# A hybrid encoder layer in which GpSimd sorts the attention's strided operand into groups of 512 columns

## The chip, the core and the metric

The kernel runs on one core of a Trainium2 chip. The metric is device microseconds of one execution. Matrix work runs on TensorE (PE; its weight loads are listed apart as PEld), elementwise work on VectorE (DVE), ScalarE (ACT) and GpSimd (POOL). Transfers are queued by SyncE (SP), by ACT and by POOL, and all of these queues end on the same 16 DMA engines. Every engine works through its own instructions in a fixed order.

## The reference, cut to what matters

One layer over 2048 tokens of width 1024: a projection, a gated linear attention (GLA, 4 heads), a dilated attention (8 heads of 64), an output projection and a mixture of 32 experts. The change touches the dilated attention only. Each head attends in three patterns, each a band of radius 64 inside classes of tokens that lie 1, 4 or 16 positions apart:

```
DILATED_PATTERNS = ((128, 1), (512, 4), (2048, 16))
for window, dilation in DILATED_PATTERNS:
    o, lse = _dilated_attention(qh, kh, vh, window, dilation)   # band inside each class i mod dilation
    outs.append(o); lses.append(lse)
w = softmax(stack(lses), axis=0)
o = einsum('pbsh,pbshd->bshd', w, stack(outs, axis=0))
```

## The kernel before, in words

Patterns are called p = 0, 1, 2 (steps of 1, 4 and 16 tokens). In each, 16 blocks of 128 queries see 256 keys (128 keys for p = 2). Queries and keys are kept with the 64 features on the partitions and the 2048 tokens along a row, in high and low parts of float32r, so that a class of p = 1 is every fourth element of a row and a class of p = 2 every sixteenth. `block(p, b)` gives the two views.

The work around the change has two stages.

The first stage (from about 240 to 757 us) computes the rest of the input projection and, in between, the maxima. `maxima(h)` goes through 24 pairs of blocks per head. A block of p = 0 or p = 1 takes two matmuls (L482, L483), a block of p = 2 one (L480); each has 128 stationary columns (the queries, `aq`) and 256 moving columns (the keys, `kk`). DVE adds a mask and takes the maximum (L490, L492), ACT sums the exponentials (L495). `pump` calls for these pairs between the matmuls of the projection (L150 to L152, L160 to L162), whose weights arrive as `wraw` and are cast by ACT (L141) and DVE (L142). POOL queues the stores of this stage and the loads of `aq` and `kk`.

The second stage (757 to about 1200 us) is the attention proper. `attention()` walks through 24 steps of two blocks per head. A step puts the mask into PSUM by a bf16 matmul (L619, L622) and adds four score matmuls (L625, L626), with the keys `ak`, `bk` stationary and the queries `aq`, `bq` moving; ACT takes the exponential (L630, L632); four steps later `att_values` multiplies by the values (L660). The GLA work is drawn in at 0.9 of its own steps per attention step: decay (L363 to L388, with POOL at L379), preparation (L750 to L763, POOL at L752), a scan (L781 to L788, on PE and DVE in turn) and the output (L802 to L852, with POOL at L835). At the end `wout_load` fetches the rows of the output projection through the buffers of `vt` (L587 to L590).

The source gives priorities by its order; the tile scheduler fixes at build time the order in which each engine works, by its own estimate of time. So a change of the source can move neighbours too.

Of the kernel before, what the change touches and what calls it, by code (L numbers as in the profile page):

```python
# [25 lines left out]
P = 128  # L26
# [64 lines left out]
def tile_trunk(ctx, tc, x, norm1_w, w_in, gfw, gfb, gbw, gbb, gnw, w_out, norm2_w, rgw, rgb, rew, reb,  # L91
# [73 lines left out]
    def duo(t, c):  # L165

        return t.rearrange("p (l c) -> p c l", c=16)[:, c - c % 2:c - c % 2 + 2, :]

    def block(p, b):

        if p == 2:
            return (lambda t: t[:, b::16]), (lambda t: duo(t, b)), am[:, 768:896], 0
# [3 lines left out]
        return (lambda t: t[:, c::st][:, P * j:P * j + P]), (lambda t: t[:, c::st][:, k0:k0 + 256]), \  # L176
            am[:, 256 * v:256 * v + 256], k0 * st // 16
# [44 lines left out]
    with ExitStack() as ca:  # L222
# [169 lines left out]
        with ExitStack() as c2:  # L392
            wp = c2.enter_context(tc.tile_pool(name="wp", bufs=2, reuse_waits="tile"))
            ev = c2.enter_context(tc.tile_pool(name="ev2", bufs=2, reuse_waits="tile"))
            lp = c2.enter_context(tc.tile_pool(name="lp", bufs=1, reuse_waits="tile"))
# [55 lines left out]
            sp = c2.enter_context(tc.tile_pool(name="sp", bufs=4, reuse_waits="tile"))  # L451
# [17 lines left out]
            def maxima(h):  # L469
                aq, kk = MX.pop(h)  # L470
                for p in range(3):
                    for b0 in range(0, 16, 2):
                        if p == 0 and b0 == 4 and h < 7:
                            maxima_load(h + 1)
                        ps = pS.tile([P, 512], F32, name="psS")
                        for i in range(2):
                            qa, ka, _, _ = block(p, b0 + i)
                            o = ps[:, i * 256:i * 256 + 256]
                            if p == 2:
                                T.matmul(o, qa(aq), kk[:, :, b0 + i::16], start=True, stop=True)  # L480
                            else:
                                T.matmul(o, qa(aq), ka(kk[:, 0]), start=True, stop=False)  # L482
                                T.matmul(o, qa(aq), ka(kk[:, 1]), start=False, stop=True)  # L483
                        for i in range(2):
# [9 lines left out]
                            je = sp.tile([P, 256], BF16, name="je", bufs=2)  # L494
                            A.activation(je[:, :n], st[:, :n], AF.Exp, bias=nm[:, col:col + 1], scale=-1.0,  # L495
# [23 lines left out]
            for n, (q, c0, nc_, dst, d0) in enumerate(jobs):  # L519
# [5 lines left out]
                if nc_ > 256 and q == 1:  # L525
                    lse = joint_lse(0, pS, lambda n: lp.tile([P, (192, 384, 384, 512)[n]], F32, name=f"lse{n}"))
# [20 lines left out]
    WO = []  # L547
    with ExitStack() as cb:
        vp = cb.enter_context(tc.tile_pool(name="vp", bufs=3, reuse_waits="tile"))
# [7 lines left out]
        BB = [[pb[e].tile([P, S], F32R, name=n) for n in ("bq", "bk")] for e in range(2)]  # L557
        for bq, bk in BB:
            for t, one in ((bq, 0.0), (bk, 1.0)):
# [1136 lines left out]
```

## Time and profile before

| | |
|---|---|
| median of 3 runs | 2322.67 us (2321.29 to 2323.6) |
| the profiled execution | 2324.34 us, span 2322.6 us |
| granted PE clock, mean | 0.954 |
| busy share PE, PEld, DVE, ACT, POOL | 91%, 74%, 61%, 55%, 44% |
| chain that ended last | PE 71%, DVE 13%, DMA 9% |

The span runs from the first to the last instruction, and the profiled execution lies 1.74 us over its span. The busy shares are means over stages with different limits. Ends of matmuls are modelled, so the pace of PE is read here from the starts: the distance from one weight load to the next is what one matmul costs in a dense stretch. [...]

### The profile page before, as it was taken

Reading aid. Unit: us, or ns where it says so; the run is one execution under the profiler, and the core shown is the slowest. Engines: PE = TensorE matmul, PEld = TensorE weight load, DVE = VectorE, ACT = ScalarE, POOL = GpSimd, SP = SyncE. Lnnn points to the kernel's source line nnn. Section 1 sums busy time; section 2 is a strip of 40 time slices with the busy share of each in tenths; the row PEclk is TensorE's granted clock in tenths of the full one; section 3 lists DMA queues with packets and bytes.
Section 4 is the critical chain, followed back from the end, with each engine's and each line's share of the span. In section 5 each row is a group of like instructions: output and inputs, shape, how many; then the busy total and the mean of one; then the engine's idle time right before and its main releaser. Section 6 shows DMA issues by size and latency. Waiting matters only on the chain.

```text
span 2322.6 us, 38346 instructions
## 1 busy us (share of the span) xinstructions
PE 2112.9 (91%) x13813; PEld 1710.3 (74%) x13813; DVE 1409.6 (61%) x2871; ACT 1281.8 (55%) x2286; POOL 1014.8 (44%) x602
## 2 busy tenths in 40 slices
PE   7999998989799799999979999588898999999975
PEld 6888897989799677878768887366665666666654
DVE  7865544545365373626434666479876777768676
ACT  5222666657486464747442333356665767676744
POOL 4766111020120111202020001388887998888866
PEclk9999999999999899999989999799999999999988
DMA  8745765575642969685454643688988999999973
GB/s 308 233 107 151 183 181 163 149 207 147 175 124 69 217 152 187 145 193 113 114 149 151 212 155 127 214 269 282 328 272 279 327 326 329 300 317 295 310 279 151
DMA packets 283475, 487.09 MB, mean 210 GB/s; under 512 B 77079, under 2 KB 155927, under 8 KB 276096
## 3 DMA queue, kind: packets, MB, share of 16 engines
q1 hardware_dynamic: 238512, 368.40, 51.1%
q0 software_dynamic: 29344, 110.03, 17.0%
q10 hardware_dynamic: 15424, 6.16, 1.1%
q8 instruction: 110, 1.80, 0.3%
q14 instruction: 85, 0.70, 0.1%
HBM read 392.01 MB, written 94.44 MB: 209 GB/s over the span
## 4 chain that ended last, share of the span: by engine, by line
PE 71%; DVE 13%; DMA 9%; issue 3%; ACT 2%; POOL 1%; SPq 1%; ACTq 0%; another core or an unknown queue 0%; DVEq 0%; POOLq 0%
DMA wraw<-in_w_in_dram 5%; PE pg L1315 4%; PE pg L1317 4%; PE pg L1316 4%; DVE wlo L991 4%; PE psm L161 3%; PE po L1302 3%; PE psm L150 3%; PE psm L152 3%; PE psm L162 3%; PE psm L151 3%; PE psm L160 3%; PE po L1076 3%; PE po L1074 3%; PE po L1078 3%
## 5 line engine op out<-in xcount | busy, mean ns | idle before, releaser
L991 POOL TENSOR_TENSOR wlo<-raw,whi 128x2048 fp32r<-128x2048 f32 x97 | 513.3, 5302 | 87.0 <-ACT whi L986 83.0
L991 DVE TENSOR_TENSOR wlo<-raw,whi 128x2048 fp32r<-128x2048 f32 x95 | 372.6, 3931 | 64.0 <-ACT whi L986 64.0
L986 ACT CAST whi<-raw 128x2048 fp32r<-128x2048 f32 x192 | 366.8, 1910 | 53.2 <-PE pg L1383 36.6
L161 PE MATMUL psm<-wl,uhi 128*128 128x256 f32 (+1 forms) x768 | 222.9, 291 | 1.1 <-DVE wl L142 1.1
L160 PE MATMUL psm<-wh,uhi 128*128 128x256 f32 (+1 forms) x768 | 222.7, 290 | 0.7 <-ACT wh L141 0.5
L162 PE MATMUL psm<-wh,ulo 128*128 128x256 f32 (+1 forms) x768 | 221.6, 289 | 0.0
L1315 PE MATMUL pg<-whi,xh 128*128 128x512 f32 x512 | 215.7, 421 | 0.7 <-ACT xh L141 0.7
L495 ACT ACTIVATE je<-st,nm 128x256 bf16<-128x256 f32 (+1 forms) x384 | 178.6, 466 | 52.3 <-DVE nm L492 50.3
L1317 PE MATMUL pg<-wlo,xh 128*128 128x512 f32 x512 | 204.7, 400 | 0.0
L1316 PE MATMUL pg<-whi,xl 128*128 128x512 f32 x512 | 204.3, 399 | 0.0
L630 ACT ACTIVATE pt<-psS 128x512 f32<-128x512 f32 x128 | 131.0, 1074 | 85.3 <-PE psS L626 46.1
L625 PE MATMUL psS<-aq,ak 128*128 128x256 f32 x384 | 172.2, 455 | 0.0
L142 DVE TENSOR_TENSOR wl<-wraw,wh 128x512 fp32r<-128x512 f32 (+1 forms) x140 | 100.6, 738 | 92.5 <-ACT wh L141 92.1
L150 PE MATMUL psm<-uhi,wh 128*128 128x512 f32 (+1 forms) x400 | 153.8, 388 | 0.3 <-ACT wh L141 0.3
L151 PE MATMUL psm<-ulo,wh 128*128 128x512 f32 (+1 forms) x400 | 153.5, 385 | 0.5 <-DVE ulo L142 0.5
L152 PE MATMUL psm<-uhi,wl 128*128 128x512 f32 (+1 forms) x400 | 152.6, 385 | 0.0
L160 PEld LDWEIGHTS psm<-wh,uhi 128*128 128x128 f32 x768 | 150.5, 196 | 1.6 <-ACT wh L141 1.0
L161 PEld LDWEIGHTS psm<-wl,uhi 128*128 128x128 f32 x768 | 150.3, 196 | 1.6 <-DVE wl L142 1.3
L162 PEld LDWEIGHTS psm<-wh,ulo 128*128 128x128 f32 x768 | 149.1, 194 | 0.0
L492 DVE CUSTOM_DVE_ANT_0 st<-psS,am 128x256 f32<-128x256 f32 x256 | 98.6, 421 | 82.9 <-PE psS L483 57.5
L626 PE MATMUL psS<-bq,bk 128*128 128x256 f32 x384 | 141.5, 374 | 0.0
L141 ACT CAST wh<-wraw 128x512 fp32r<-128x512 f32 (+1 forms) x144 | 85.1, 623 | 97.3 <-DMA wraw<-in_w_in_dram 85.6
(420 smaller groups left out, 5097.1 us busy)
## 6 DMA issues: line engine op xcount, KB each, us to landing
raw<-in_expert_w_gate_dram SPq DMA_DIRECT2D x128, 512.0 KB
raw<-in_expert_w_up_dram SPq DMA_DIRECT2D x128, 512.0 KB
raw<-in_expert_w_down_dram SPq DMA_DIRECT2D x64, 1024.0 KB
wraw<-in_w_in_dram SPq DMA_DIRECT2D x128, 256.0 KB
xt<-in_x_dram SPq DMA_DIRECT2D x32, 512.0 KB
aq<-s_q POOLq DMA_DIRECT2D x8, 1024.0 KB, 8.3
kk<-s_khi POOLq DMA_DIRECT2D x16, 512.0 KB, 13.4
ak<-s_khi SPq DMA_DIRECT2D x16, 512.0 KB
```

What stands on the lines that cost most here:

```text
L150: T.matmul(ps[:m, ts], wh[:, k, m0:m0 + m], uh[:, k, ts], start=(k == 0), stop=False)
L151: T.matmul(ps[:m, ts], wh[:, k, m0:m0 + m], ul[:, k, ts], start=False, stop=False)
L152: T.matmul(ps[:m, ts], wl[:, k, m0:m0 + m], uh[:, k, ts], start=False, stop=(k == KD - 1))
L160: T.matmul(ps[:, :n], uh[:, k, sl], wh[:, k, :n], start=(k == 0), stop=False)
L161: T.matmul(ps[:, :n], uh[:, k, sl], wl[:, k, :n], start=False, stop=False)
L162: T.matmul(ps[:, :n], ul[:, k, sl], wh[:, k, :n], start=False, stop=(k == KD - 1))
L495: A.activation(je[:, :n], st[:, :n], AF.Exp, bias=nm[:, col:col + 1], scale=-1.0, accum_out=zt[:, col:col + 1])
L986: (A.copy if high is A else high.tensor_copy)(hi, raw)
L991: low.tensor_tensor(lo, raw, f32(hi), op=ALU.subtract)
L1315: T.matmul(pgt[n], xh[:, k], hi[:, 2 * n + kk], start=(k == 0), stop=False)
L1316: T.matmul(pgt[n], xl[:, k], hi[:, 2 * n + kk], start=False, stop=False)
L1317: T.matmul(pgt[n], xh[:, k], lo[:, 2 * n + kk], start=False, stop=(k == KD - 1))
```

## The change

GpSimd copies the moving operand of p = 1 and p = 2 into a tile `grp` of 128 partitions, 2 parts and 512 columns, in which the columns of each class lie side by side. There are four groups per pattern and head: one class of p = 1 each, or four classes of p = 2. Matmuls then read their 256 moving columns contiguously. The stationary operand is read as before, every fourth or sixteenth element. In the first stage this is the keys (`in_order` in `maxima`), in the second the queries (`in_order(h, p, g)`, called two steps before the group is used). Each stage has two `grp` buffers.

So that a step stays within one group, the steps of p = 1 now take blocks (4c+1, 4c+2) and (4c, 4c+3) of one class, and p = 2 runs c = 0 to 7. Blocks 4c and 4c+3 have different masks, so every second step of p = 1 takes two mask matmuls of 256 columns instead of one of 512. The values of p = 2 are taken step by step.

To find room for `grp`: `st` has 3 buffers instead of 4 and the exponential is written over it (`je` is gone), the pool `lp` is gone (its use goes to `tab`), `lz` becomes an `oe` buffer, `vt` has 2 buffers instead of 3, and `aq`, `bq` become one tile `qq`. The DVE memset of `bq` (2 x 2048) is gone.

```
+                def in_order():
+                    if todo_:
+                        p, g = todo_.pop(0)
+                        ready[p, g] = t = pa.tile([P, 2, 512], F32R, name="grp")
+                        if p == 1:
+                            G.tensor_copy(t, kk.rearrange("p e (m c) -> p e c m", c=4)[:, :, g])
+                        else:
+                            G.tensor_copy(t.rearrange("p e (c l) -> p e c l", c=4),
+                                          kk.rearrange("p e (l c) -> p e c l", c=16)[:, :, 4 * g:4 * g + 4])
...
                 for p in range(3):
                     for b0 in range(0, 16, 2):
+                        if (p, b0) in ((0, 8), (0, 12)) or (p and b0 % 4 == 0):
+                            in_order()
...
-                                T.matmul(o, qa(aq), kk[:, :, b0 + i::16], start=True, stop=True)
+                                T.matmul(o, qa(aq), kg.rearrange("p e (c l) -> p e c l", c=4)[:, :, (b0 + i) % 4], start=True, stop=True)
                             else:
-                                T.matmul(o, qa(aq), ka(kk[:, 0]), start=True, stop=False)
-                                T.matmul(o, qa(aq), ka(kk[:, 1]), start=False, stop=True)
+                                for e in range(2):
+                                    T.matmul(o, qa(aq), (kg if p else kk)[:, e, near], start=(e == 0), stop=(e == 1))
...
-        vp = cb.enter_context(tc.tile_pool(name="vp", bufs=3, reuse_waits="tile"))
+        vp = cb.enter_context(tc.tile_pool(name="vp", bufs=2, reuse_waits="tile"))
...
+        def in_order(h, p, g):
+            qq = ATT[h][2]
+            ATT["grp", h, p, g] = t = vp.tile([P, 2, 512], F32R, name="grp", bufs=2)
+            if p == 1:
+                G.tensor_copy(t, qq.rearrange("p e (m c) -> p e c m", c=4)[:, :, g])
+            else:
+                for x in range(2):
+                    G.tensor_copy(t[:, :, 256 * x:256 * x + 256].rearrange("p e (y l) -> p e y l", y=2),
+                                  qq.rearrange("p e (l c) -> p e c l", c=16)[:, :, 8 * x + 2 * g:8 * x + 2 * g + 2])
...
-                T.matmul(sv[:, e], ks(ak), qs(aq), start=False, stop=False, skip_group_check=True)
-                T.matmul(sv[:, e], ks(bk), qs(bq), start=False, stop=True, skip_group_check=True)
+                for w, kt in enumerate((ak, bk)):
+                    T.matmul(sv[:, e], ks(kt), (qg if p else qq)[:, w, near], start=False, stop=(w == 1), skip_group_check=True)
...
+                    n = t % 24 - 6
+                    if n >= 0 and n % 2 == 0 and n < 16:
+                        in_order(h, 1 + n // 8, n // 2 % 4)
```

The build puts the copies into POOL's queue as follows. Around the first stores of the values in the first stage, POOL's rows before are these (`s_...` are scratch tensors in memory, `kk_1912` is one of the two key tiles):

```order
L413 DMA s_gq<-ef 128x512 x2
L413 DMA s_gk<-ef 128x512 x2
L448 DMA s_v<-et 128x4x256
L464 DMA aq<-s_q 128x2048
L135 DMA kk_1912<-s_khi 64x2048 x2
```

At the same place POOL's rows now read (the key tiles are called `kk_1909` and `kk_1910`, and L442 is the former L448):

```order
L476 COPY grp<-kk_1909 128x1024 x2
L442 DMA s_v<-et 128x4x256
L476 COPY grp<-kk_1909 128x1024 x2
L474 COPY grp<-kk_1910 128x1024
L135 DMA kk_1909<-s_khi 64x2048 x2
```

Copies now stand in front of the stores and behind them, in the one queue. In the second stage, at the output of the first GLA head and the decay of the second, POOL's rows before are these (`tab` holds the decay tables, `vr` the GLA norm):

```order
L363 DMA lr<-s_lr 96x512 x2
L379 TENSOR_TENSOR tab<-tab 128x512 x2
L363 DMA lr<-s_lr 96x512 x2
L835 TENSOR_TENSOR vr<-vr,mhalf 128x4
L379 TENSOR_TENSOR tab<-tab 128x512 x2
```

Now they are (L374 is the former L379, L864 the former L835):

```order
L589 COPY grp<-qq 128x1024
L374 TENSOR_TENSOR tab<-tab 128x512 x2
L358 DMA lr<-s_lr 96x512
L589 COPY grp<-qq 128x1024
L358 DMA lr<-s_lr 96x512
L864 TENSOR_TENSOR vr<-vr,mhalf 128x4
L592 COPY grp<-qq 128x2x256 x2
L374 TENSOR_TENSOR tab<-tab 128x512 x2
```

Here copies and GLA instructions stand in turn. On PE, a step of p = 2 in the same stage reads before (L619 the mask, L625 and L626 the scores, L660 the values of an earlier step):

```order
L660 MATMUL pso<-pt,vt 64x2x64
L619 LDWEIGHTS identb
L619 MATMUL psS<-am,identb 128x2x128
L625 MATMUL psS<-aq,ak 128x256
L626 MATMUL psS<-bq,bk 128x256
```

and now (L648 the mask, L657 the scores, L691 the values, L831 a GLA matmul):

```order
L691 MATMUL pso<-pt,vt 64x2x64 x4
L648 LDWEIGHTS identb
L648 MATMUL psS<-am,identb 128x2x128
L831 MATMUL psg<-qd,ki 64x64 x3
L657 MATMUL psS<-grp,ak 128x256
L657 MATMUL psS<-grp,bk 128x256
```

The scores of a step no longer follow its mask at once; other work is put between, and some scores of p = 2 stand in the next head's steps of p = 0.

## Rows read from the trace of the kernel before

**Rows 1.** Windows by stage: us, busy (instructions) of each engine, PE clock, DMA share, GB/s.
```profile
240.00:757.00 517.00, 478.92 (x3128) 460.21 (x3126) 265.89 (x1067) 332.43 (x1027) 85.53 (x110) 0.96 0.56 154
757.00:1200.00 443.00, 409.44 (x4431) 340.93 (x4431) 211.36 (x463) 253.83 (x432) 70.00 (x63) 0.95 0.70 155
1200.00:1217.00 17.00, 2.20 (x8) 1.43 (x8) 5.33 (x19) 3.67 (x5) 0.43 (x2) 0.54 0.89 256
```

**Rows 2.** Timeline of PEld, a pair of p = 1: start us, us, engine, line.
```profile
266.60 0.19 PEld L161 LDWEIGHTS psm<-wl,uhi 128*128 128x128 f32 x1
266.72 0.31 PEld L482 LDWEIGHTS psS<-kk,aq 128*128 128x128 f32 x1
266.94 0.33 PEld L483 LDWEIGHTS psS<-kk,aq 128*128 128x128 f32 x1
...
267.41 0.34 PEld L483 LDWEIGHTS psS<-kk,aq 128*128 128x128 f32 x1
267.65 0.21 PEld L162 LDWEIGHTS psm<-wh,ulo 128*128 128x128 f32 x1
267.86 0.21 PEld L160 LDWEIGHTS psm<-wh,uhi 128*128 128x128 f32 x1
```

**Rows 3.** Timeline of PEld, a pair of p = 2 in the first stage.
```profile
282.87 0.52 PEld L480 LDWEIGHTS psS<-kk,aq 128*128 128x128 f32 x2
283.29 0.20 PEld L160 LDWEIGHTS psm<-wh,uhi 128*128 128x128 f32 x1
283.49 0.21 PEld L161 LDWEIGHTS psm<-wl,uhi 128*128 128x128 f32 x1
```

**Rows 4.** Timeline of PEld, a strided step of the second stage.
```profile
922.43 0.29 PEld L625 LDWEIGHTS psS<-aq,ak 128*128 128x128 f32 x1
922.63 0.31 PEld L626 LDWEIGHTS psS<-bq,bk 128*128 128x128 f32 x1
...
923.06 0.32 PEld L626 LDWEIGHTS psS<-bq,bk 128*128 128x128 f32 x1
923.48 0.11 PEld L619 LDWEIGHTS <-identb 128*128 128x128 bf16 x1
```

**Rows 5.** Timeline of PEld, a contiguous step (p = 0) of the second stage.
```profile
934.80 0.19 PEld L625 LDWEIGHTS psS<-aq,ak 128*128 128x128 f32 x1
934.92 0.19 PEld L626 LDWEIGHTS psS<-bq,bk 128*128 128x128 f32 x1
935.15 0.10 PEld L619 LDWEIGHTS <-identb 128*128 128x128 bf16 x1
```

**Rows 6.** Chain that ended last, second stage: start us, us, what.
```profile
754.72 1.78 DVE bq L561
...
845.11 5.61 issue
850.72 1.29 POOL tab L379
...
950.16 5.64 issue
```

**Rows 7.** Single lines: instructions, ns min/median/max, first and last start us.
```profile
L443 POOL TENSOR_TENSOR et<-et,nw x8: 2332/2404/2462, 229.8 to 654.5; 128x1024 f32<-128x1024 f32 x8
L560 POOL MEMSET bq<- x2: 1801/1804/1808, 605.5 to 752.4; 64x2048 f32 x2
L991 POOL TENSOR_TENSOR wlo<-raw,whi x97: 4495/5167/6696, 1439.6 to 2246.0; 128x2048 fp32r<-128x2048 f32 x97
L142 DVE TENSOR_TENSOR wl<-wraw,wh x140: 616/689/2501, 22.2 to 728.2; 128x512 fp32r<-128x512 f32 x124, 128x576 fp32r<-128x576 f32 x16
```

**Rows 8.** Waits: who waited for whom, us in total, times, longest us.
```profile
ACT wh L141 <- DMA wraw<-in_w_in_dram: 69.2, 22, 15.5
...
POOL vr L835 <- DVE vr L834: 74.1, 12, 16.2
```

**Rows 9.** Timeline at the end of the second stage, SP and DVE.
```profile
1201.30 1.41 SPq L587 DMA_DIRECT2D vt<-in_w_out_dram  x1
1208.50 1.23 DVE L590 TENSOR_TENSOR bk<-vt,bk 128x1024 fp32r<-128x1024 f32 x1 [2.77 <-ACT bk L589]
```

More of the change, by code (lines that the diff above doesn't have):

```diff
@@ L470, in maxima @@
                 aq, kk = MX.pop(h)
+                todo_ = [(p, g) for p in (1, 2) for g in range(4)]
+                ready = {}
+                def in_order():
[7 more added lines that the diff above has]
+                                          kk.rearrange("p e (l c) -> p e c l", c=16)[:, :, 4 * g:4 * g + 4])
                 for p in range(3):
                     for b0 in range(0, 16, 2):
+                        if (p, b0) in ((0, 8), (0, 12)) or (p and b0 % 4 == 0):
+                            in_order()
+                        kg = ready.get((p, b0 // 4))
                         if p == 0 and b0 == 4 and h < 7:
@@ L587, in wout_load @@
             SY.dma_start(raw, w_out[0, k * P:(k + 1) * P, :])
-            t = pb[k // 4].tile([P, 2, D], F32R, name=("aq", "ak", "bq", "bk")[k % 4])
+            if k % 4 < 2:
+                WQ[k] = pb[k // 4].tile([P, 2, S], F32R, name="qq") if k % 4 == 0 else WQ[k - 1]
+                t = WQ[k][:, k % 4].rearrange("p (a n) -> p a n", a=2)
+            else:
+                t = pb[k // 4].tile([P, 2, D], F32R, name=("ak", "bk")[k % 2])
             A.copy(t[:, 0], raw)
@@ L601, in att_steps @@
                     yield h, 0, (b, b + 8)
-                for b in range(8):
-                    yield h, 1, (b, b + 8)
-                for c in (0, 4, 1, 5, 2, 6, 3, 7):
+                for c in range(4):
+                    yield h, 1, (4 * c + 1, 4 * c + 2)
+                    yield h, 1, (4 * c, 4 * c + 3)
+                for c in range(8):
                     yield h, 2, (c, c + 8)
@@ L609, in att_scores @@
                 ATT[h] = att_load(h)
-            aq, ak, bq, bk = ATT[h]
+            ak, bk, qq = ATT[h]
+            qg = ATT.get(("grp", h, p, blocks[0] // 4 if p == 1 else blocks[0] // 2))
             ps = psS.tile([P, 512], F32, name="psS")
@@ L616, in att_scores @@
             mask = lambda e, k: m[e][:, None, :].to_broadcast([P, k, n])
-            if p or blocks[0] not in (0, 7):
+            if blocks[0] % 4 if p == 1 else p or blocks[0] not in (0, 7):
                 ATT["last"] = T.matmul(sv[:, :, o:o + n], identb, mask(0, 2), start=True, stop=False, skip_group_check=True)
@@ L657, in att_values @@
             if p == 2:
-                val = [(b // 8, b, (m, b % 8), pts[e // 2][:, 256 * (e % 2) + 64 * m:256 * (e % 2) + 64 * m + 64]) for m in range(2) for e, b in enumerate(blocks)]
+                val = [(b // 8, b, (m, b % 8), pts[0][:, 256 * e + 64 * m:256 * e + 64 * m + 64]) for m in range(2) for e, b in enumerate(blocks)]
             for hf, b, d, src in val:
@@ L892, in tile_trunk @@
         work2 = all_gla()
[L893 to L895 removed]
+        work3 = joint_lse(1, psS, lambda n: gs.tile([P, 4, P], F32, name=("oe", "oe", "sg", "sg")[n]).rearrange("p i n -> p (i n)"))
         cred = 0.0
```

54 lines of the change are left out of this document (22 added, 32 removed).

## The prediction

> **What bounds the kernel now.** I read the windows by stage first. In the two stages that the change touches PE is busy 478.92 of 517 us and 409.44 of 443 us, over 92% each, while DVE, ACT and POOL stay under two thirds [rows 1]. So PE's pace is the first thing to look at, and I took it from the timeline of its weight loads, as the distance from start to start. A plain projection matmul (both operands contiguous, 128 stationary and 256 moving columns) takes 266.72 - 266.60 = 0.12 us. A pair of p = 1 has four matmuls with both operands strided; from its first load to the second plain load behind it the trace takes 267.86 - 266.72 = 1.14 us, five distances of 0.21 to 0.24 [rows 2]. So a strided matmul costs nearly twice a plain one.
>
> The question on which everything hangs is which of its two operands makes it slow, because the change makes only the moving one contiguous. The edges of the group answer it. When the first strided load starts at 266.72, the matmul ahead of it is a plain one, which needs 0.12 us of the array; the next load still comes only at 266.94, 0.22 us later. What lasted was the strided load itself. At the other edge the load of 267.65 is a plain one and the matmul that runs beside it is the last strided one; the next load comes after 0.21 us. There it was the moving stream that lasted. So each operand alone takes about 0.21 to 0.22 us when strided, and they run side by side. The same holds in the second stage: 0.20 us from the first to the second strided load although only a mask of 256 bf16 columns streams there [rows 4], against 0.12 us between the loads of a contiguous step [rows 5].
>
> I then looked at the waits and the chain for what else could end last: ACT waits 69.2 us in all for the projection weights [rows 8], and twice the chain of the second stage stands about 5.6 us before a POOL instruction of the GLA decay (L379) [rows 6].
>
> **The matmuls.** After the change the moving stream is contiguous and the stationary load is not. A strided matmul is then paced by its load, 0.22 us, and only the last one of a group, whose neighbour behind it loads plainly, falls to 0.12 us.
> - Pair of p = 1, first stage: 4 x 0.22 + 0.12 = 1.00 instead of 1.14, saved 0.14 us. There are 8 heads x 8 pairs = 64: 9.0 us.
> - Pair of p = 2, first stage: from 282.87 to 283.29 two loads take 0.42 and the last stream 0.20, 0.62 together [rows 3]. Now 0.42 + 0.12 = 0.54, saved 0.08 us, 64 times: 5.1 us.
> - Step of the second stage: from the first strided load to the next mask's load 923.48 - 922.43 = 1.05 us, of which the last stream with its load takes 0.42 [rows 4]; a contiguous end takes 935.15 - 934.92 = 0.23 [rows 5]. The last matmul's load stays (0.21) and its stream falls to about 0.11, so 0.10 us is saved, in 8 x 16 = 128 steps: 12.8 us.
>
> That is 26.9 us at the full clock. [...] Not all of it lies on the path: in bursts of `pump` the pairs are paced by DVE and ACT, and during the scan of GLA by DVE. I take seven tenths, 17 us; the bounds are 0 and 24.5.
>
> [...]
>
> **The copies.** POOL gains 64 copies of 128 x 1024 in each stage (those of p = 2 in the second stage as two halves). No strided copy is in this trace. The nearest rows are a two-input operation on 128 x 1024 at 2.40 us and a memset of 2048 elements a partition at 1.80 us, so 0.9 us for 1024; the dearest is the two-input operation of the last stage, up to 6.70 us for 2048 beside a busy DVE, 3.3 us for 1024 [rows 7]. I take 2.4 us, the row of the same size. That is 154 us of POOL in each stage, on top of 86 and 70 us [rows 1]: under half of its time, so POOL's throughput does not bind. A group lasts two steps; 443 us over 192 steps is 2.3 us a step, so a copy has 4.6 us, and it is hidden as long as nothing queues ahead of it.
>
> [...]
>
> What queues behind the copies is GLA's own POOL work. At both places of rows 6 PE, through DVE, waits for two pairs of L379, and in the new order a copy stands ahead of each pair. If each pair comes one copy late, that is 2 x 2 x 2.4 = 9.6 us; the bounds are 0 (the engine stood 5.6 us there for "issue", in which a copy could fit) and 20 (a pow and a second copy ahead too). DVE operations with two SBUF inputs may be held up by a POOL operation: L142 has a median of 0.69 and a maximum of 2.50 us [rows 7]. In the first stage they are a job ahead of their use, which hides them.
>
> **The small edits.** The memset of `bq` stands on the chain with 1.78 us [rows 6] and is gone: -1.8 (0 to -3.5, if that of the other buffer shows too). With two `vt` buffers the last rows of the output projection come later by about one DVE subtraction, 1.23 us [rows 9], in a stretch in which PE is idle anyway [rows 1]: +1.2 (0 to 6, one more transfer). The smaller pool of `st` costs nothing in the sum: where DVE stalls on it, ACT is held by weights that have not landed (69.2 us, rows 8), and that wait ends when they land. Bound 0 to 4. The extra mask matmuls stream the same number of columns. `lz`, `lp` and `je` go without a wait that I can find.
>
> **The sum.** -17 - 1.8 + 9.6 + 1.2 = -8.0 us. The profiled execution took 2324.34 us for a span of 2322.6, within 0.1% of the median of 2322.67; off the median the forecast is 2314.7, rounded 2315 us. Its own range, from the bounds of its terms, is 2296 to 2325.
>
> **Rivals.**
> 1. *The strided load does not pace PE after all* (it overlaps once the stream beside it is plain). Then a pair of p = 1 takes 5 x 0.12 = 0.60 instead of 1.14, a pair of p = 2 0.36 instead of 0.62, and a step saves 4 x 0.10 and some: 64 x 0.54 + 64 x 0.26 + 128 x 0.4 = 102 us, times 0.9 for the clock and 0.7 for the path: -64, with the other terms -55, so 2268 us. For it speaks that no row shows a strided load beside a plain stream for longer than one matmul; against it both edges of rows 2 and 4. [...]
> 2. *Nothing to be seen.* The gain at the edges of groups goes into waits that end elsewhere: for the weights in the first stage (69.2 us, rows 8), for GLA's scan in the second. 2322 us. For it speaks how thin each gain is (0.08 to 0.14 us per group); against it that PE is busy 92%.
> 3. *Slower: POOL's queue holds the copies back.* L835 waits for DVE 12 times, 74.1 us in all, 6.2 us each [rows 8]. Today nobody needs what stands behind it. In the new order copies do, and scores wait for the copies. If half of each such wait reached PE, the 16 of them (4 heads x 4 quarters) would cost 16 x 3.1 = 50 us; with the other terms +42, so 2365 us; a quarter gives 2340. It decides from 8 / 16 = 0.5 us per wait on. Against it: the scheduler has put the scores of p = 2 far behind their masks, so some delay is covered, and PE's order ties both sides together.
>
> **Chances.** Forecast 0.38, rival 1 0.10, rival 2 0.22, rival 3 0.30. What a measurement of this kernel can tell from no change is about 0.2%, 4.6 us. Part of the forecast's own spread falls inside that (0.03, while as much of rival 2 is a small gain), so: faster 0.48, same 0.22, slower 0.30. The range that should hold 8 times in 10 reaches down to near rival 1 and up to the middle of rival 3: 2270 to 2350.
>
> **What the profile will show.** If the step on the matmuls is right, the weight loads of scores in a strided group still stand 0.21 to 0.22 us apart, and only the distance behind the last one falls to about 0.12. If rival 1 holds, all of them stand at 0.12. The copies should take 0.9 to 3.3 us; PE waiting for POOL copies should be few us in all, and tens of us if rival 3 holds, mostly behind the former L835. The forecast is wrong if the first stage does not shorten by some 8 to 13 us, or if the second one changes by more than 15 us either way.

## The result: 2.6% slower, and the profile after

The changed kernel takes 2383.74 us in the median (2377.19 to 2388.59) against 2322.67 us of the kernel before (2321.29 to 2323.60); the ratio is 1.0262, with a 95% interval of 1.0228 to 1.0295. One more execution of the kernel before ran in a slow state, took 2848.24 us, and is not compared. The forecast was 2315 us, with a range of 2270 to 2350.

Three marks cut every run's profile alike: the first mask matmul of the attention, the last value matmul, and the first matmul of the output projection. These are their rows in the changed kernel (operation, count, duration in ns, first and last start):

```profile
L651 PE MATMUL psS<-am,identb x96: 268/282/421, 763.7 to 1223.9; 128*128 128x256 bf16 x96
...
L691 PE MATMUL pso<-pt,vt x1856: 192/271/476, 769.6 to 1243.0; 128*64 128x128 f32 x70, 128*64 128x64 f32 x52, 128*64 128x32 f32 x37, 128*64 128x96 f32 x27
...
L1101 PE MATMUL po<-qq,mh x128: 392/395/796, 1275.2 to 1495.4; 128*128 128x512 f32 x128
```

The windows between the marks, columns as in [rows 1], after:

```profile
240.00:763.70 523.70, 476.05 (x3123) 454.62 (x3122) 296.83 (x1068) 330.34 (x1027) 220.06 (x176) 0.95 0.56 156
763.70:1243.00 479.30, 436.63 (x4461) 358.51 (x4463) 233.59 (x459) 252.17 (x426) 200.01 (x155) 0.93 0.60 135
1243.00:1275.20 32.20, 2.44 (x16) 1.53 (x12) 6.55 (x21) 7.86 (x8) 5.05 (x4) 0.52 0.74 208
```

and cut at the same marks, before:

```profile
240.00:758.80 518.80, 478.96 (x3129) 460.25 (x3128) 267.66 (x1069) 333.29 (x1027) 85.53 (x110) 0.96 0.56 155
758.80:1198.80 440.00, 409.19 (x4431) 340.81 (x4431) 209.02 (x460) 252.03 (x429) 70.00 (x63) 0.95 0.70 155
1198.80:1217.10 18.30, 2.44 (x17) 1.53 (x13) 5.95 (x21) 4.71 (x6) 0.43 (x2) 0.57 0.83 238
```

The first stage ends 4.9 us later, the attention takes 39.3 us more, the boundary behind it 13.9 us more, and the third stage, which is not touched, 5.3 us less. POOL went from 70 to 200 us in the attention, about as foreseen; DVE, whose instructions are nearly the same (459 and 460), went from 209 to 234. That was not foreseen, and the next rows show where it sits. DVE's lines in the attention (shapes, count, busy us, mean ns, idle time ahead of them and what ended it), before:

```profile
L788 DVE SCALAR_TENSOR_TENSOR ss<-ss,dec,psg 64x128 f32<-64x128 f32 x124 | 43.9, 354 | 4.0
...
L382 DVE TENSOR_TENSOR_SCAN tab<-rm,tab 64x512 f32<-64x512 bf16 x24 | 35.6, 1483 | 24.6 <-POOL tab L379 24.3
L840 DVE SCALAR_TENSOR_TENSOR oe<-oe,vr,sg 128x128 f32<-128x128 f32 x64 | 18.2, 347 | 16.3 <-POOL vr L835 16.3
```

and after:

```profile
L817 DVE SCALAR_TENSOR_TENSOR ss<-ss,dec,psg 64x128 f32<-64x128 f32 x124 | 43.9, 354 | 4.0
...
L377 DVE TENSOR_TENSOR_SCAN tab<-rm,tab 64x512 f32<-64x512 bf16 x24 | 42.0, 1748 | 10.3 <-POOL tab L374 10.0
L869 DVE SCALAR_TENSOR_TENSOR oe<-oe,vr,sg 128x128 f32<-128x128 f32 x64 | 36.7, 632 | 7.7 <-POOL vr L864 7.7
```

The scan of GLA's states reads one input from PSUM (psg) and keeps its 354 ns to the nanosecond. The decay scan (L377) and the gating (L869) read both large inputs from SBUF and grew by 18% and 82% in the mean. The gatings one by one (min/median/max in ns), before and after:

```profile
L840 DVE SCALAR_TENSOR_TENSOR oe<-oe,vr,sg x64: 336/347/354, 862.3 to 1195.8; 128x128 f32<-128x128 f32 x64
L869 DVE SCALAR_TENSOR_TENSOR oe<-oe,vr,sg x64: 327/346/2465, 871.5 to 1241.6; 128x128 f32<-128x128 f32 x64
```

The median has not moved. Twenty of the 64 took 1.0 us or more, and two of them over 2.4. Nor did every operation with two SBUF inputs grow: the one on qd (L782) takes 764 ns in the mean, against 766 before. So the operation with an input in PSUM has 354 and 354 ns, and of those with both inputs in SBUF the gating has 347 and 632. All twenty long gatings ran beside a POOL operation on 512 or more columns (L592, L781, L374, L617) for at least 87% of their time; the 35 with no POOL operation beside them took at most 354 ns.

How that reaches PE is seen at one place of the attention. Timelines of DVE, POOL and PE, after (start us, us; in brackets the idle time ahead):

```profile
971.98 9.38 DVE L377 TENSOR_TENSOR_SCAN tab<-rm,tab 64x512 f32<-64x512 bf16 x4 [4.99 <-POOL tab L374]
981.40 0.75 DVE L362 TENSOR_SCALAR tab<-psg,gb 128x512 f32<-128x512 f32 x1
...
973.13 3.01 POOL L589 CAST grp<-qq 128x1024 fp32r<-128x1024 f32 x1
...
976.58 2.47 POOL L589 CAST grp<-qq 128x1024 fp32r<-128x1024 f32 x1
...
982.20 1.75 PE L831 MATMUL psg<-qd,ki 64*64 64x64 f32 x26 [5.11 <-DVE tab L362]
```

Four scans take 9.38 us (at their median of 1.22 us they would take 4.9) while two copies run beside them, and the copies take 3.01 and 2.47 us instead of 2.07 in the median. DVE's L362, which empties a psg buffer, stands behind the scans, PE's next GLA matmul waits 5.11 us for it, and PE does nothing else from 977.09 to 982.20.

### The profile page after: what moved, and what is told of

It is laid out like the page before. It is cut to its first block, busy times and chain, and to the rows that moved or that the text cites. A ratio compares the mean times of both kernels' runs of the same rounds, so it can differ in the third digit from the quotient of the medians.

```text
span 2375.4 us, 38472 instructions
## 1 busy us (share of the span) xinstructions
PE 2133.1 (90%) x13845; PEld 1719.8 (72%) x13845; DVE 1458.7 (61%) x2869; ACT 1281.3 (54%) x2286; POOL 1284.1 (54%) x762
## 4 chain that ended last, share of the span: by engine, by line
PE 46%; DVE 11%; DMA 3%; ACT 3%; issue 2%; SPq 1%; POOL 1%; ACTq 0%; another core or an unknown queue 0%; DVEq 0%; POOLq 0%
PE pg L1342 4%; PE psS L657 4%; PE pg L1343 4%; PE pg L1344 4%; PE po L1329 3%; DVE wlo L1018 3%; PE pso L691 3%; PE po L1101 3%; PE po L1103 3%; PE po L1105 3%; PE pg L1409 2%; PE pg L1411 2%; PE pg L1410 2%; PE pse L1304 1%; DVE tab L377 1%
## 5 line engine op out<-in xcount | busy, mean ns | idle before, releaser
L1018 DVE TENSOR_TENSOR wlo<-raw,whi 128x2048 fp32r<-128x2048 f32 x95 | 365.0, 3851 | 67.9 <-ACT whi L1013 66.8
L505 ACT ACTIVATE st<-st,nm 128x256 f32<-128x256 f32 (+1 forms) x384 | 178.5, 466 | 72.3 <-DVE nm L503 70.3
L142 DVE TENSOR_TENSOR wl<-wraw,wh 128x512 fp32r<-128x512 f32 (+1 forms) x140 | 125.8, 915 | 99.1 <-ACT wh L141 98.6
L691 PE MATMUL pso<-pt,vt 128*64 128x128 f32 (+3 forms) x1856 | 130.1, 261 | 0.2
L589 POOL CAST grp<-qq 128x1024 fp32r<-128x1024 f32 x32 | 69.0, 2160 | 107.7 <-PE psS L657 95.7
## 6 DMA issues: line engine op xcount, KB each, us to landing
aq<-s_q POOLq DMA_DIRECT2D x8, 1024.0 KB, 11.6
```

Source lines behind the costliest of these rows:

```text
L505: A.activation(st[:, :n], st[:, :n], AF.Exp, bias=nm[:, col:col + 1], scale=-1.0, accum_out=zt[:, col:col + 1])
L691: T.matmul(po[64 * hf:64 * hf + 64][(slice(None),) + d], vt[:, b], src, start=(d[0], hf) not in begun, stop=True, skip_group_check=True)
L1018: low.tensor_tensor(lo, raw, f32(hi), op=ALU.subtract)
```

## The experiments

All numbers in us. "Start" is the first mask matmul, "attention" from there to the last value matmul, "boundary" from there to the first output projection, each of the run's one profile; the ratio is to the kernel before. Eight of these kernels (after, e4, e9, e12 to e16) work in the same order up to about 650 us, and their attention starts at 759.9 to 767.2; e9 has the order of the changed kernel up to the output projection. Marks of single profiles scatter by some us, and differences as small are not read as effects.

| run | start | attention | boundary | ratio, 95% interval |
|---|---|---|---|---|
| before | 758.8 | 440.0 | 18.3 | 1 |
| after | 763.7 | 479.3 | 32.2 | 1.0262 [1.0228, 1.0295] |
| e1 strided, no copies | 759.9 | 447.7 | 6.5 | 1.0008 [0.9988, 1.0027] |
| e2 contiguous, no copies | 755.9 | 442.0 | 6.7 | other third stage |
| e3 copies unread | 800.0 | 448.9 | 32.0 | 1.0252 [1.0208, 1.0295] |
| e4 four buffers at the tail | 760.4 | 489.3 | 20.5 | 1.0238 [1.0198, 1.0278] |
| e5 both contiguous | 719.9 | 416.3 | 7.1 | other data |
| e6 thin copies | 740.1 | 436.0 | 30.4 | other third stage |
| e7 copies on ACT | 751.4 | 443.7 | 31.9 | 1.0069 [1.0046, 1.0091] |
| e8 copies on DVE | 770.4 | 432.5 | 31.8 | 1.0097 [1.0071, 1.0122] |
| e9 own pool | 759.9 | 477.4 | 12.7 | 1.0148 [1.0123, 1.0172] |
| e10 ACT, then DVE, own pool | 746.0 | 441.2 | 6.3 | 0.9907 [0.9884, 0.9930] |
| e11 copies twice | 830.2 | 583.9 | 22.1 | 1.0939 [1.0908, 1.0971] |
| e12 decay on DVE | 765.4 | 473.8 | 32.5 | 1.0203 [1.0098, 1.0309] |
| e13 order kept | 767.0 | 485.7 | 30.9 | 1.0275 [1.0236, 1.0314] |
| e14 GLA off POOL | 764.3 | 477.5 | 32.3 | 1.0267 [1.0221, 1.0314] |
| e15 only copies on POOL | 764.1 | 480.2 | 31.0 | 1.0260 [1.0205, 1.0316] |
| e16 the same, copies on DVE | 767.2 | 435.3 | 30.6 | 1.0055 [1.0013, 1.0098] |

**e1, the change without copies.**
```
-    in_order(...)                       # both stages
-    ... kg[:, e, near] ... qg[:, w, near]
+    ... kk.rearrange("p e (m c) -> p e c m", c=4)[:, :, g][:, e, near] ...   # qq alike; p = 2 with c=16
```


> The changed kernel without its 128 copies: all scores read the moving operand with its step of 4 or 16, as before; the new order of steps, the tiles qq, the two vt buffers and st instead of je stay. Theory A (the copies' time on POOL does the harm: DVE operations with two SBUF inputs are held up and POOL's own GLA work comes late): second stage 443 to 450 us, boundary about 30 us since that is vt's, total about 2330 to 2340 us. Rival B (the new order of the steps and the scheduler's answer to it do the harm): second stage 470 to 490 us, total 2365 to 2385 us.

The total is that of before. The new order of steps costs the attention 7.7 us, but the boundary shrinks to 6.5 us although there are two vt buffers: my reason for the long boundary, those buffers, fell here.

**e2, contiguous and no copies.**
```
-    kg = ready.get((p, b0 // 4))
+    kg = kk[:, :, 512 * g:512 * g + 512]    # qg of qq alike
```


> As the run without copies, same order of instructions on every engine, but the scores of p = 1 and p = 2 read 512 contiguous columns of kk and qq in place (other columns than the computation asks for, so the output is another). Only the form of the moving stream differs between the two. My theory (a strided weight load of 0.22 us paces PE, a contiguous stream saves only at the end of a group): 10 to 27 us less than the run without copies in the two stages together. Rival (the stream paces): 60 us or more less.

Every engine has the same order as in e1, so the difference is the moving stream's form alone: the first output projection comes at 1204.6 instead of 1214.1, 9.5 us. (Its third stage took 1244.8 us, as other scores send tokens to other experts.) The rival's 60 us are out. Weight loads around a pair of p = 1, in e1:

```profile
268.42 1.02 PEld L492 LDWEIGHTS psS<-kk,aq 128*128 128x128 f32 x4
269.35 0.21 PEld L160 LDWEIGHTS psm<-wh,uhi 128*128 128x128 f32 x1
269.56 0.21 PEld L161 LDWEIGHTS psm<-wl,uhi 128*128 128x128 f32 x1
```

and in e2:

```profile
273.35 1.01 PEld L492 LDWEIGHTS psS<-kk,aq 128*128 128x128 f32 x4
274.26 0.21 PEld L160 LDWEIGHTS psm<-wh,uhi 128*128 128x128 f32 x1
274.40 0.19 PEld L161 LDWEIGHTS psm<-wl,uhi 128*128 128x128 f32 x1
```

Four strided loads need 0.93 and 0.91 us, and only the distance behind them fell, 0.21 to 0.14. The pair goes from 1.14 to 1.05 us, not to 1.00.

**e5, the stationary operand contiguous as well.**
```
-    return (lambda t: t[:, c::st][:, P * j:P * j + P]), ...
+    return (lambda t: t[:, P * b:P * b + P]), ...          # p = 2 alike
```


> As the run that reads contiguous moving columns in place without copies, in the same order of instructions, but the stationary operand of the scores of p = 1 and p = 2 is 128 contiguous columns too (other columns than the computation asks for, so the output is another and with it what the experts of the third stage get; only the first two stages are compared). Theory (the strided weight load of 0.22 us paces PE): loads now stand 0.12 us apart, 0.10 us less for 4 matmuls of 64 pairs of p = 1, 2 of 64 pairs of p = 2 and 4 of 128 steps, 90 us at the full clock and some 40 to 70 us of the time up to the first output projection, which came at 1204.6 us. Rival (neither operand's step was what held PE back in wall time): under 15 us less.

Again e2's order on every engine. The output projection begins at 1143.3 us, 61.3 us earlier. The same kind of pair in e5:

```profile
263.45 0.66 PEld L492 LDWEIGHTS psS<-kk,aq 128*128 128x128 f32 x4
264.04 0.19 PEld L152 LDWEIGHTS psm<-uhi,wl 128*128 128x128 f32 x1
264.16 0.19 PEld L150 LDWEIGHTS psm<-uhi,wh 128*128 128x128 f32 x1
```

0.59 us for four loads instead of 0.91. So strided loads did pace PE: of the 70.8 us between e1 and e5, the moving one alone gives 9.5. All these loads have 128 columns. The converse, a contiguous stationary beside a strided moving operand, was not run.

**e3, the same copies, unread.** Two small tiles keep them alive.
```
     G.tensor_copy(t, ...)                   # as in the change
+    G.tensor_copy(seen[:, n:n + 1], f32(t)[:, 0, 0:1])
-    ... kg[:, e, near] ...                  # scores read strided, as e1
```


> As the run without copies (scores read strided), but all 128 copies run on POOL; nobody waits for them but a one-column POOL copy that reads one column of each. So PE cannot wait for a copy and gains nothing from one. [...] Rival C (what costs is that PE and the order of the scores hang on the copies): second stage within 8 us of the run without copies.

A miss for theory A, as e1's expectation has it (the copies' time on POOL does the harm): the gating takes 718 ns here, yet the attention takes 448.9 us, 1.2 more than e1. DVE's delays alone did not reach PE where nothing on PE hung on a copy. (PE's order differs from the changed kernel's too; see what stays open.) The first stage, though, ran 40 us longer than e1's (start at 800.0 against 759.9); there copies no longer wait for PE, and what PE waited for is not shown here.

**e4, four buffers for the output projection's rows.**
```
-    raw = vp.tile([P, D], F32, name="vt")
+    raw = vp.tile(..., name="vt") if k % 2 else vp.tile(..., name="grp", bufs=2)
```


> The changed kernel, but the eight rows of the output projection are loaded in turn into a grp and a vt buffer, four buffers instead of two. Theory (two buffers serialise load, ACT cast and subtraction behind the attention): the boundary between the second and the third stage falls from 30 to about 17 us, total 2363 to 2377 us, some 10 to 13 us under the changed kernel. Rival (the boundary is late because attention and its scan end late): boundary stays 28 to 30 us.

The boundary fell to 20.5 us, the attention took 489.3, and the total did not move: 2381.67 us, where 2363 to 2377 were expected. Why the attention took 10 us more than the changed kernel's is not shown.

**e9, the grp buffers in a pool of their own, allocated last.**
```
+    gq = cb.enter_context(tc.tile_pool(name="gq", bufs=2, reuse_waits="tile"))   # behind gs
-    t = vp.tile([P, 2, 512], F32R, name="grp", bufs=2)
+    t = gq.tile([P, 2, 512], F32R, name="grp")
```


> The changed kernel with the two grp buffers of the second stage in a pool of their own, allocated last, instead of inside vp. Theory (with grp in vp the first tiles of the third stage, gl among them, lie where the two vt buffers are, so their loads stand behind all eight rows of the output projection; that is the 24 us at the boundary): boundary from the last value matmul to the first output projection 6 to 12 us instead of 32, total 2358 to 2366 us, still slower than before. Rival (the boundary is late because of two vt buffers or a late GLA): 25 us or more at the boundary, total within 6 us of the changed kernel.

Boundary 12.7 instead of 32.2, total 2359.98. SP's queue at the end of the second stage, in the changed kernel:

```profile
1250.47 9.66 SPq L610 DMA_DIRECT2D vt<-in_w_out_dram  x4
1260.23 0.38 SPq L1082 DMA_DIRECT2D gl<-s_gla  x1
```

and in e9:

```profile
1238.97 0.36 SPq L611 DMA_DIRECT2D vt<-in_w_out_dram  x1
1239.38 1.11 SPq L701 DMA_DIRECT2D s_att<-acc  x2
1240.59 1.02 SPq L1083 DMA_DIRECT2D gl<-s_gla  x2
1244.55 0.33 SPq L611 DMA_DIRECT2D vt<-in_w_out_dram  x1
```

In the changed kernel gl stands behind all rows of the output projection, each waiting for a buffer; in e9 between them. Only the place of 8 KB per partition was changed. Which tile of the third stage overlaps which buffer is not shown.

**e6, thin copies.**
```
-    G.tensor_copy(t, kk...[:, :, g])
+    G.tensor_copy(t[:, :, 0:4], kk...[:, :, g, 0:4])     # all 128 alike, two zeroed tiles as buffers
```


> The changed kernel with all 128 copies and all that hangs on them (PE waits for POOL, POOL for PE), but each copy moves 8 columns of its 1024; the rest of the two buffers is set to zero once, so scores of p = 1 and p = 2 are other ones and only the first two stages are compared. Theory A (the time that POOL spends copying, while DVE and POOL's GLA work are held up): from the first mask of the attention to the first output projection 448 to 462 us, as without copies (454), against 511 of the changed kernel; DVE L869 back at 0.35 us. Rival D (waits between PE and POOL and the order that goes with them): 495 us or more.

Between the two expectations, for two reasons that run against each other: the attention takes 436.0 us, 4.0 less than before, so with copies this short the waits between PE and POOL cost nothing that can be seen; the boundary stays at 30.4, as grp is in vp.

**e11, every copy twice.**
```
-    G.tensor_copy(t, ...)
+    for _ in range(2):
+        G.tensor_copy(t, ...)
```


> The changed kernel with every POOL copy made twice, so 276 us of copies in the two stages become some 550. Theory A: the attention of the second stage takes 436 us with thin copies (37 us of POOL there... few columns each), 479 us with copies of 2 us; with twice the time it grows at least as much again, 520 to 570 us, and DVE's L869 mean rises above 0.63 us; total 2440 us or more. Rival (the form of the order alone, whatever the copies take): within 10 us of 479.

With thin, whole and doubled copies the attention takes 436.0, 479.3 and 583.9 us: it grows with the copies' time on POOL, and more than in proportion. That time acts in two ways that these runs do not separate: on the chip, and through the scheduler, which reckons with it. On PE, scores follow a group of masks with no other matmul of the attention between them in 192 of 193 cases with thin copies, in 114 of 191 in the changed kernel and in 68 of 192 here.

**e7 and e8, the copies on ACT and on DVE.**
```
-    G.tensor_copy(t, ...)
+    A.copy(t, ...)            # e7        V.tensor_copy(t, ...)    # e8
```


> The changed kernel with all its copies on ACT instead of POOL. Theory A: DVE's operations with two SBUF inputs are back at their durations of before (L869 0.35 us, scans 1.5 us), the stretch from the first mask to the first output projection is 450 to 470 us (511 in the changed kernel), total 2315 to 2340 us. Rival D (waits on copies, whichever engine makes them): 490 us or more, total above 2360 us.

> The changed kernel with all its copies on DVE instead of POOL. Theory A: no second engine works on SBUF beside DVE for the copies, so its other operations keep their durations; each copy adds 0.7 to 1.2 us of DVE: stretch 455 to 485 us, total 2320 to 2355 us. Rival D: 490 us or more, total above 2360 us.

ACT needs as long for a copy as POOL (2.04 and 1.98 us in the mean for those of the first stage, read in e10, against 2.06 and 2.05 on POOL in the changed kernel), and the attention still takes 443.7 us; DVE needs 1.22 us (e8, mean), and it takes 432.5, although DVE then does all of it. Both boundaries stay at 32 (e7's expected stretch was missed by that).

**e12, e13 and e14, three ways in which POOL might do it.**
```
-    G.tensor_tensor(tb[:, sl], tb[:, sl], ta[:, sl], op=ALU.subtract)
+    V.tensor_tensor(tb[:, sl], tb[:, sl], ta[:, sl], op=ALU.subtract)     # e12, e14
-    G.tensor_tensor(ke, kv, dec...)
+    V.tensor_tensor(ke, kv, dec...)                                       # e14
+    with tc.issue_after(ATT["score"].ins):   # e13: masks and values behind the last score
```


> The changed kernel with the subtraction of GLA's decay (L374, 16 times 1.27 us) on DVE instead of POOL, so that no decay stands in POOL's queue behind a copy; the copies stay on POOL. Theory A1 (DVE is held up while POOL copies, its scans and its other two-input operations above all): the attention still takes 470 to 490 us (479), scans L377 still above 1.6 us in the mean, PE still waits some 5 us twice for DVE's L362. Theory A2 (POOL's queue: the decay comes late because copies stand ahead of it): attention at 455 us or less.

> The changed kernel with copies on POOL, but PE's order among the attention's matmuls is held to the order of the steps: the masks of a step and the values that follow stand behind the scores of the step before. In the changed kernel 114 of 191 groups of masks are followed by their own scores before other attention work, here 192 of 194, as with thin copies. Theory O (with copies that are long on POOL the order itself, in which scores stand behind later masks and values and GLA's matmuls in front of them, costs the time): the attention takes 455 us or less, though scans L377 still take above 1.55 us in the mean. Theory A (POOL's copying beside DVE, and copies that really come late, cost it): 470 us or more, and then PE waits for POOL's grp by tens of us.

> The changed kernel, copies on POOL, with GLA's two large POOL operations of the second stage (subtraction of the decay L374 and the product with dec L781, 28 operations of 1.3 us) on DVE; only the small pow (16 times) still stands in POOL's queue between the copies. Theory Q (one queue: GLA's POOL work stands behind copies that wait for PE to give a buffer back, while PE waits for what follows from that work): attention at 455 us or less, though DVE has some 25 us more to do beside the copies. Theory A1 (DVE is slower while POOL copies): 470 us or more. In between: both.

None brought the time back: 473.8, 485.7, 477.5. The decay on DVE gained 5.5 us. The order of masks and scores by itself is not the cause: in e13 scores follow all 192 groups of masks. Nor did PE wait for grp by tens of us in e13, which A had expected.

**e15 and e16, both at once, and the engine alone.**
```
     e13 + e14
-    G.dma_start(lr, lrS[:, sl])
+    SY.dma_start(f32(lr), lrS[:, sl])
-    G.tensor_copy(t, qq...)
+    V.tensor_copy(t, qq...)                  # e16 only
```


> [...] Theory A1 (POOL's copies slow DVE, and GLA with it): attention 470 us or more. Theory Q+O (POOL's queue and PE's order together): 455 us or less.

> The run before with the copies of the second stage on DVE, all else alike: the same PE order rule, GLA's operations on DVE, lr on SP's queue. DVE then has the copies (76 us) and GLA's operations (24 us) beside its own. Theory A1: attention about 435 to 450 us, at least 25 us less than with the copies on POOL, although DVE has the more to do. Theory Q+O: within 10 us of the run with copies on POOL, or longer than it.

e15 joins e13 and e14 and loads lr by SP's queue; e16 differs from it in the engine of the second stage's copies. The two are 44.9 us apart; in both the copies of the first stage are POOL's. DVE's lines in the attention, e15:

```profile
L377 DVE TENSOR_TENSOR_SCAN tab<-rm,tab 64x512 f32<-64x512 bf16 x24 | 39.6, 1649 | 0.3
L871 DVE SCALAR_TENSOR_TENSOR oe<-oe,vr,sg 128x128 f32<-128x128 f32 x64 | 31.4, 550 | 9.7 <-POOL vr L866 9.6
```

and e16:

```profile
L377 DVE TENSOR_TENSOR_SCAN tab<-rm,tab 64x512 f32<-64x512 bf16 x24 | 29.2, 1217 | 0.4
L871 DVE SCALAR_TENSOR_TENSOR oe<-oe,vr,sg 128x128 f32<-128x128 f32 x64 | 18.2, 348 | 9.6 <-POOL vr L866 8.5 <-DMA qd<-s_gq 1.2
```

What PE waited for in e15 (us, times, longest):

```profile
PE psg L833 <- DVE tab L362: 16.5, 3, 5.7
PE psS L652 <- ACT pt L662: 11.1, 2, 9.6
PE psS L649 <- ACT pt L662: 11.1, 4, 10.2
PE psg L812 <- DVE ss L819: 8.3, 1, 8.3
```

The wait for L362 does not occur in e16's list. With POOL's queue empty of GLA's large operations and the order of masks and scores held, the engine that copies still makes the difference. The windows of the attention, e15 and e16 (columns as above):

```profile
764.10:1244.30 480.20, 423.57 (x4463) 350.19 (x4463) 246.00 (x487) 250.68 (x426) 159.84 (x115) 0.92 0.60 136
767.20:1202.50 435.30, 409.09 (x4463) 345.47 (x4463) 277.06 (x581) 250.40 (x427) 30.66 (x23) 0.96 0.67 152
```

PE is idle for 56.6 us in e15 and for 26.2 in e16. What the lower clock costs is an estimate from the granted clocks of these windows: (1 - 0.92) x 480.2 - (1 - 0.96) x 435.3 = 21 us more, good to some 5 us as the clocks are rounded. It is an upper one. In the kernel before, the plain loads at a granted clock of 0.50 (365.1 to 368.1 us) stand 0.21 us apart and at 1.00 (369 to 372 us) 0.12, but the strided loads just ahead, at 0.50 too (364.5 to 365.1 us), stand 0.21 to 0.22 apart, no more than in [rows 2]. The two together, 51 us by this estimate, cover the whole difference. The way over DVE shows in a part of it. The four scans ahead of e15's first pause for L362, and the same four in e16:

```profile
853.39 8.43 DVE L377 TENSOR_TENSOR_SCAN tab<-rm,tab 64x512 f32<-64x512 bf16 x4
860.14 4.93 DVE L377 TENSOR_TENSOR_SCAN tab<-rm,tab 64x512 f32<-64x512 bf16 x4
```

These four took 3.50 us longer than in e16, and all 24 scans of the attention 10.4 us (39.6 against 29.2); the three pauses make 16.5 us. The two longest pauses of e15, 10.2 us at 920.5 and 9.6 at 1040.4, are of another kind: PE waits for ACT's exponentials, and ACT, which has a store of GLA's output to issue first (L889, at 919.0 and 1038.9), for transfers to land, though DVE had ended the gating ahead of it at 900.9 and 1024.2. ACT's rows there:

```profile
919.46 2.81 ACT L662 ACTIVATE pt<-psS 128x512 f32<-128x512 f32 x3 [12.89 <-DMA gv<-s_gv]
...
1039.28 3.70 ACT L662 ACTIVATE pt<-psS 128x512 f32<-128x512 f32 x4 [10.81 <-DMA s_gla<-oe]
```

The two kernels differ in more than the copying engine: their masks and scores have one order, but the scheduler put the values and GLA's matmuls elsewhere between them. What the copies do on the chip and what the scheduler makes of them is not separated.

**e10, what the causes point to.** Copies of the first stage on ACT, where DVE is needed, of the second on DVE, where GLA is; grp in its own pool.
```
     e9 +
-    G.tensor_copy(t, kk...)       -    G.tensor_copy(t, qq...)
+    A.copy(t, kk...)              +    V.tensor_copy(t, qq...)
```


> Copies of the first stage on ACT, of the second on DVE, none on POOL, and the grp buffers of the second stage in a pool of their own. If the three causes are right and add up: attention begins at about 751 us as with copies on ACT, 433 us of attention as with copies on DVE, boundary of 7 to 12 us; first output projection at 1191 to 1200 us (1217 before), total 2296 to 2312 us, faster than both. Rival (the gains were given back by something not seen yet): 2320 us or more.

2304.95 us, ratio 0.9907 with an interval of 0.9884 to 0.9930: faster than both kernels, by 0.9% than before. The total is in the expected range; the attention, 441.2 us, missed the expected 433 by 8. Its windows:

```profile
240.00:746.00 506.00, 470.19 (x3128) 449.50 (x3128) 277.05 (x1070) 442.29 (x1091) 86.35 (x111) 0.98 0.57 160
746.00:1187.20 441.20, 409.35 (x4461) 345.48 (x4463) 279.19 (x552) 251.02 (x426) 76.05 (x61) 0.95 0.66 149
1187.20:1193.50 6.30, 1.36 (x14) 0.85 (x10) 0.00 (x0) 2.64 (x3) 2.71 (x2) 0.71 0.75 233
```

## Why the prediction was wrong

e1 and e2 split the change. In us, from the table; the third stage's -5.3 makes the +52.8 between the two spans:

| | start | attention | boundary | sum |
|---|---|---|---|---|
| new order and pools (e1 - before) | +1.1 | +7.7 | -11.8 | -3.0 |
| contiguous stream (e2 - e1) | -4.0 | -5.7 | +0.2 | -9.5 |
| copies on POOL (after - e2) | +7.8 | +37.3 | +25.5 | +70.6 |

**The step that failed is the copies'**: "it is hidden as long as nothing queues ahead of it", with +9.6 us (0 to 20) for late GLA pairs. The duration was right, 2.05 to 2.22 us a copy in the mean against 2.4 taken, and they were hidden from the scores: PE's weight loads waited 1.0 us in all for a copy. But the copies cost 70.6 us, 37.3 of them in the attention and 25.5 at the boundary, and e15 and e16 put 44.9 us of attention on the engine that makes them. The step looked for the copies' cost in queues only. It named the other way, that DVE operations with two SBUF inputs may be held up by a POOL operation [rows 7], and closed it with the first stage, where such work is a job ahead of its use. In the second stage the same kind of operation is GLA's chain, on which PE waits in its own order, and no term of the sum stood for it. The row that should have raised the question is in the same group: L142 with a median of 0.69 and a maximum of 2.50 us. That hold-up is measured (in the kernel before the two L142 of 2.50 us, at 377.5 and 513.3 us, ran beside POOL's L443, and the 125 with no POOL operation beside them took at most 0.76; the gating is shown above), and so are pauses of PE behind it (9.8 us for L362 in the changed kernel). That it carries the whole cost is not shown.

What the 39.3 us of the attention consist of can be read from the windows. PE's idle time went from 30.8 (440.00 - 409.19) to 42.7 us. The granted clock went from 0.95 to 0.93, and (1 - 0.93) x 479.3 - (1 - 0.95) x 440.0 makes 11.6 us more lost to the clock, by the same upper estimate as for e15 and e16, good to some 5 us. Part of that stands with the new pauses: the granted clock is 0.80 in the 10 us from 984, behind the pause of 5.1 us at 977, and 0.66 in those from 1094, which hold the pause of 4.7 us at 1096. The contiguous stream gives 5.7 back, e1's order takes 7.7. Some 14 us of PE's busy time are left by this estimate, and they go with PE's order. The window of e13, where that order is held:

```profile
767.00:1252.70 485.70, 432.31 (x4461) 356.55 (x4463) 233.56 (x458) 253.68 (x426) 197.47 (x152) 0.91 0.59 134
```

Without the clock's share, by the same estimate, PE is busy for 432.31 - 0.09 x 485.7 = 388.6 us there (385.2 in e15, by its window above), and for 436.63 - 0.07 x 479.3 = 403.1 in the changed kernel. e13 loses it again in pauses, 53.4 us, and in the clock.

**The matmuls** were right in mechanism and too large in size: -17 foreseen, -9.5 measured. No run shows the 24.5 us of which the 17 are seven tenths, nor rival 1's factor of 0.9 for the clock; in their place the rows give 26.9 us, and e2 showed 9.5 less than e1. The loads stay 0.21 to 0.23 apart, as the first sign of the list wanted, and in the changed kernel too (eight loads, two pairs):

```profile
269.69 1.94 PEld L494 LDWEIGHTS psS<-grp,aq 128*128 128x128 f32 x8
271.54 0.21 PEld L161 LDWEIGHTS psm<-wl,uhi 128*128 128x128 f32 x1
271.67 0.19 PEld L162 LDWEIGHTS psm<-wh,ulo 128*128 128x128 f32 x1
```

Two pairs in a row share one edge, so counting 64 edges for pairs of p = 1 [rows 2] was too many, and an edge gives 0.09 us, not 0.14. In the second stage 5.7 us over 128 steps is 0.04 a step, not 0.10 [rows 4]. The first stage's 4.0 us and this 5.7 are each no more than single profiles scatter; their sum and the shorter distance at each edge carry the reading.

**The tail** was foreseen at +1.2 (0 to 6) because of two vt buffers; it is +13.9, and the buffers are not the reason (e1 has two and 6.5 us). The 8 KB of grp inside vp are, for 19.5 us of the 25.5 (e9). **The memset** of bq gave nothing that can be seen: e1's attention starts 1.1 us later than before. The extra mask matmuls and the new order, taken at 0, cost the attention 7.7 us in e1. The forecast's own range, 2296 to 2325, is not what its bounds add up to: they give -28 to +30 us, 2295 to 2353, which the result lies outside of as well.

**The rivals.** Rival 1 (the load does not pace) fell with e5, rival 2 with the result. Rival 3 had the sign and two thirds of the size (+42 of +61), but not the way: neither were the copies late for PE, nor was the wait behind L835 the place; e12 to e15 took POOL's queue apart without getting the time back. What it held against itself is what the kernel shows: the scheduler did put scores far behind their masks.

**What stays open:** e3 has the same copies and the slowest gating of all single-copy runs, and its attention lost 1.2 us. So DVE's delays alone do not make the harm. Two things set e3 apart: nothing on PE hangs on a copy, and with that the scheduler kept PE's order. In e3 scores follow 191 of 192 groups of masks, and in every kernel whose attention is under 450 us at least 184 of the 192 to 194; in the changed kernel it is 114 of 191, in e12 and e14 128 of 191 and 137 of 185. e13 and e15 have that order held and take 485.7 and 480.2 us all the same, but not the places of the values and of GLA's matmuls. Whether PE loses the time through DVE's held-up operations (16.5 us of pauses for L362 in e15), through such places, or through ACT's exponentials and stores is not isolated. A run with e16's orders on every engine but DVE and POOL, and the copies on POOL, would show it.

## What to carry to other kernels

Copying to another engine is not free because that engine is idle: ask which of its neighbour's operations read two operands from SBUF (here the gating went from 347 to 632 ns in the mean, the state's scan with an operand in PSUM stayed at 354), whether those lie on a chain that the bound engine waits for in its own order, and what order the scheduler makes of a slow copy. Here the same copies cost the attention 45 us more on POOL than on DVE, the busier engine. Where two operands of a matmul were slow side by side, making one of them fast gave only the edges of each group, 9.5 us of the 70.8 for both (e2, e5); and of the 25.5 us that the copies cost at the boundary, 19.5 came from where their buffers lie (e9).

## What the hardware showed that I had not expected

- In dense stretches a float32 matmul of 256 columns takes 0.21 to 0.24 us with a strided stationary operand ([rows 2]; four loads in 0.91 us with a contiguous moving one, e2), 0.21 at the one edge where only the moving one is strided ([rows 2], e1), and 0.12 with both contiguous ([rows 2]). The moving one made contiguous alone gave 9.5 us of the 70.8 that both gave (e1, e2, e5).
- A strided copy of 128 x 1024 takes 2.01 to 2.07 us on POOL (medians of the changed kernel), 1.98 to 2.04 on ACT (means, e10) and 1.17 to 1.22 on DVE (means, e16 and e8).
- Beside copies on POOL a DVE operation with both inputs in SBUF, the gating, grew from 347 to 632 ns in the mean (single ones to 2465), one with an input in PSUM not at all (354); another with both in SBUF, L782, did not grow either (766 and 764). With the copies on DVE and POOL all but empty (e16) it stays at 348; where POOL keeps GLA's operations it is 439 (e8) and 489 (e10), and the attention is fast even so.
